# z and u of an input projection by one level of Strassen products, v computed next and kept in DRAM

## The chip, the core and the metric

The kernel runs on one core of a Trainium2 chip. Its five instruction queues work at the same time and wait for each other through semaphores: TensorE (PE: matmuls, with PEld for its weight loads), VectorE (DVE), ScalarE (ACT), GpSimd (POOL) and SyncE (SP, which here only starts DMAs). Every queue runs its instructions in the order in which the program holds them. The metric is the device time of one execution in microseconds (us), lower is better.

## The reference, cut to what matters

One decoder layer on x of 1024 tokens by 1024 columns, in f32. The change touches the first product and what uses its parts:

```python
h = x @ w_in                     # (1024, 1024) @ (1024, 2560)
q, k, v = h[:, 0:512], h[:, 512:1024], h[:, 1024:1536]
u = gelu(h[:, 1536:2048]);  z = gelu(h[:, 2048:2560])
A = dilated_attention(rope(q), rope(k), v)
B = u * (tril(w_s) @ layernorm(z) + b_s)        # 8 chunks of 128 tokens, 8 groups of 64 columns
x = LN1(alpha * x + concat(A, B) @ w_o)
# then a gated feed-forward, LN2, a gated per-layer input, LN3
```

## The kernel before, in words

Every f32 product is made of three matmuls (`mm3`, lines 131 to 134): each operand is split into a high part, which ACT copies in a matmul type (`copy`, line 111), and a low part, the rest, which DVE or POOL subtracts (`split`, line 117); the matmuls are high by high, high by low and low by high. Such a triple on 128 by 128 by 512 is called a group below.

Tokens come in eight tiles of 128. The transposed x is loaded in two halves of the 1024 contracted columns (kh 0 and 1) and four pairs of token tiles (tp 0 to 3), 512 KB each (`load_x`, line 193). The weight w_in comes in five blocks of 512 columns (4 is z, 3 is u, 2 is v, 1 is k, 0 is q) and four slices of 256 contracted rows, 512 KB each (`load_w`, line 125). All split parts of x stay in SBUF until q is done.

The order of the dense work on PE is: z (64 groups, into all eight PSUM banks), u (64 groups, pair by pair through `dense_pair`; the spatial gating `gmlp(0)` and two transposes `gm_T` are woven into its last quarter), the half of the output projection that needs only B (`wo_low`), v (64 groups), k, q, and then attention. While u is computed, DVE and ACT normalise z (`z_norm`: statistics, a power on POOL, two DVE operations, a split), eight times. v is split from PSUM straight into the tiles VL and VP. The work is laid out by hand: the program's text sets the order in each queue (`manual_schedule`), and buffers of a pool are taken in turn, so that a taker waits for the last reader of the buffer before. Pools that matter here: `raw` (2 buffers of 4 KB per partition, for loads), `w` (12, for split weights), `pg` (24 pages), `L` (3 large ones); in PSUM `A` (2 buffers of two banks: zA, ups, vps, kps), `B` (2 banks), `D0` and `D1`.

Of the kernel before, what the change touches and what calls it, by code (L numbers as in the profile page):

```python
# [30 lines left out]
DM = 1024  # L31
# [20 lines left out]
def hybrid_layer(ctx, tc, x, xT, pT, pos, w_in, ln_z_g, ln_z_b, w_sT, b_sT, w_o,  # L52
# [14 lines left out]
    def page(shape, dt, name):  # L67
        return pool.tile(shape, dt, name=name, tag="pg", bufs=24)

    def wpage(shape, dt, name):  # L70
        return pool.tile(shape, dt, name=name, tag="w", bufs=12)

    def rawpage(shape):
        return pool.tile(shape, F32, name="raw", tag="raw", bufs=2)
# [40 lines left out]
    def split(hi, lo, src, hi_eng=ACT, lo_eng=DVE):  # L115
        copy(hi_eng, hi, src)
        lo_eng.tensor_tensor(lo, src, hi.bitcast(F32), OP.subtract)  # L117

    def load_w(src, shape, name, hi_eng=ACT, lo_eng=POOL, parts=1, alloc=wpage):
        raw = rawpage(shape)  # L120
        hi = alloc(shape, F32R, name + "h")
        lo = alloc(shape, F32R, name + "l")
        n = shape[1] // parts
        for q in range(parts):
            SP.dma_start(raw[:, q * n:(q + 1) * n], src[:, q * n:(q + 1) * n])
        for q in range(parts):
            sl = slice(q * n, (q + 1) * n)
            split(hi[:, sl], lo[:, sl], raw[:, sl], hi_eng, lo_eng)
        return hi, lo
# [6 lines left out]
    def bcast(dst, vec, n, eng=SP):  # L136
        eng.dma_start(dst, bass.AP(tensor=vec.tensor, offset=vec.offset, ap=[[0, 128], [1, n]]))
        return dst
# [40 lines left out]

    x1acc_d = dram.tile([NT, 128, DM], F32, name="x1acc_d")  # L180
    x1_d = dram.tile([NT, 128, DM], F32, name="x1_d")
    hid_d = dram.tile([NG, 128, 7, 512], F32, name="hid_d")

    xh = [[None] * 4 for _ in range(2)]
    xl = [[None] * 4 for _ in range(2)]

    def load_x(kh, tp, parts=1):
        raw = page([128, 4, 256], F32, "xraw")
        xh[kh][tp] = page([128, 4, 256], F32R, "xh")
        xl[kh][tp] = page([128, 4, 256], F32R, "xl")  # L190
        st = 4 // parts
        for k in range(0, 4, st):
            SP.dma_start(raw[:, k:k + st, :], xT[kh, tp, :, k:k + st, :])
        for k in range(0, 4, st):
            split(xh[kh][tp][:, k:k + st, :], xl[kh][tp][:, k:k + st, :], raw[:, k:k + st, :])

    def xs(a, k, i):
        return a[k // 4][i // 2][:, k % 4, (i % 2) * 128:(i % 2 + 1) * 128]

    class Loader:  # L200
        def __init__(self, srcs, shape, name, lo_eng=POOL):
# [10 lines left out]
    def group(g, lo_eng=DVE):  # L212
        return Loader([w_in[g, s] for s in range(4)], [128, 2, 512], "wi", lo_eng)

    W = []
    raw0, raw1 = rawpage([128, 2, 512]), page([128, 4, 256], F32, "xraw")
    W.append((wpage([128, 2, 512], F32R, "wih"), wpage([128, 2, 512], F32R, "wil")))
    xh[0][0], xl[0][0] = page([128, 4, 256], F32R, "xh"), page([128, 4, 256], F32R, "xl")
    SP.dma_start(raw0[:, 0:1], w_in[4, 0][:, 0:1])
    SP.dma_start(raw1[:, 0:1], xT[0, 0, :, 0:1, :])  # L220
    SP.dma_start(raw0[:, 1:2], w_in[4, 0][:, 1:2])
    for k in range(1, 4):
        SP.dma_start(raw1[:, k:k + 1], xT[0, 0, :, k:k + 1, :])
    split(W[0][0][:, 0:1], W[0][1][:, 0:1], raw0[:, 0:1])
    split(xh[0][0][:, 0:1], xl[0][0][:, 0:1], raw1[:, 0:1])
    split(W[0][0][:, 1:2], W[0][1][:, 1:2], raw0[:, 1:2])
    for k in range(1, 4):
        split(xh[0][0][:, k:k + 1], xl[0][0][:, k:k + 1], raw1[:, k:k + 1])
    W.append(load_w(w_in[4, 1], [128, 2, 512], "wi", lo_eng=DVE, parts=2))
    load_x(0, 1)  # L230
    load_x(0, 2)
    load_x(0, 3)
    W.append(load_w(w_in[4, 2], [128, 2, 512], "wi"))
    load_x(1, 0)
    load_x(1, 1)
    W.append(load_w(w_in[4, 3], [128, 2, 512], "wi"))
    load_x(1, 2)
    load_x(1, 3)

    gbz = page([128, 2, 512], F32, "gbz")  # L240
    bcast(gbz[:, 0, :], ln_z_g, 512)
    bcast(gbz[:, 1, :], ln_z_b, 512)
    SP.dma_start(ident, c_id)
    SP.dma_start(bs, b_sT)
    SP.dma_start(mask, c_mask)

    Wu = group(3, POOL)
    Wu.load(4)

    zt = [psA("zA"), psA("zA")]  # L250
    for _ in range(10):
        PE.matmul(zt[0][:, 0:512], warm[:, 0:128], warm, start=True, stop=True)
    zbanks = [zt[0][:, 0:512], zt[0][:, 512:1024], zt[1][:, 0:512], zt[1][:, 512:1024],
              psB("zB"), psB("zB2"), psD("zD"), psD("zD2")]
    for kh in range(2):
        for tp in range(4):
            for k in range(4 * kh, 4 * kh + 4):
                mh = W[k // 2][0][:, k % 2, :]
                ml = W[k // 2][1][:, k % 2, :]
                for i in (2 * tp, 2 * tp + 1):  # L260
                    mm3(zbanks[i], xs(xh, k, i), xs(xl, k, i), mh, ml, k == 0, k == KB - 1)

    W = Wu
    znh = big([128, NT, 512], F32R, "znh")
    znl = big([128, NT, 512], F32R, "znl")
    z_prev = []

    def z_norm(i, zz, stats):
        ln_dve(zz, zz, *stats, gbz[:, 0, :], gbz[:, 1, :])
        split(znh[:, i, :], znl[:, i, :], zz)  # L270

    for tp in range(4):
        z = page([128, 2, 512], F32, "z")
        if tp < 2:
            ACT.activation(z.rearrange("p a b -> p (a b)"), zt[tp], AF.Gelu)
        else:
            for t in range(2):
                ACT.activation(z[:, t, :], zbanks[2 * tp + t], AF.Gelu)
        for t in range(2):
            stats = ln_stats(z[:, t, :], 512)  # L280
            if z_prev:
                z_norm(*z_prev.pop())
            z_prev.append((2 * tp + t, z[:, t, :], stats))
    z_norm(*z_prev.pop())

    def dense_pair(j, W, pa):
        for k in range(KB):
# [8 lines left out]
        for _ in gen:  # L296
            pass

    u = big([128, NT, 512], F32, "u")
    def gmlp(ch):  # L300
        for g in range(H):
            ps = (psB if g % 2 else psD)("gps")[:, 0:256]
# [21 lines left out]

    WOL = Loader([w_o[4 + k] for k in range(4)], [128, 1024], "wol", DVE)
    for j in range(4):
        pa = psA("ups")
        g = dense_pair(j, W, pa)
        if j == 3:
            gg = gmlp(0)  # L330
            for n in range(4):
                next(g)
                next(gg)
                next(gg)
                if n % 2:
                    WOL.load(1)
            run(gg)
            next(g)
            next(g)
            WOL.load(1)  # L340
            gm_T(0)
            next(g)
            gm_T(1)
        run(g)
        if j == 0:
            wsr = rawpage([128, H, 128])
            SP.dma_start(wsr, w_sT)
            POOL.affine_select(wsr, wsr, pattern=[[0, H], [1, 128]], compare_op=OP.is_ge, fill=0.0,
                               base=0, channel_multiplier=-1)
            wsh = wpage([128, H, 128], F32R, "wsh")  # L350
            wsl = wpage([128, H, 128], F32R, "wsl")
            split(wsh, wsl, wsr)
        if j == 1:
            WOL.load(1)
        ACT.activation(u[:, 2 * j:2 * j + 2, :].rearrange("p a b -> p (a b)"), pa, AF.Gelu)

    Wv = group(2)
    Wv.load(1)
    xrs = {}

    def load_xr(i):
# [18 lines left out]
    for i in range(NT):  # L380
        if i == 1:
            run(gmlp(1))
        if i == 2:
            Wv.load(1)
        if i == 6:
            rp = page([128, 5, NT, 8], F32, "rp")
            posi, inv = rp[:, 3, 0, :].bitcast(I32), rp[:, 4, 0, :]
            SP.dma_start(posi, pos)
            bcast(inv, c_inv, 8)
        wo_low(i)  # L390
        if i + 2 < NT:
            gm_T(i + 2)
    Wv.load(2)
    ACT.dma_start(x1acc_d[NT - 1], xrs.pop(NT - 1))

    posf, ang, nn = rp[:, 0, 0, :], rp[:, 1], rp[:, 2]
# [24 lines left out]
            VP[kb] = page([128, H, 128], F32R, "VP")  # L421
        return VP[kb]

    W = Wv
    Wk = group(1)
    for j in range(4):
        pa = psA("vps")
        run(dense_pair(j, W, pa))
        if j == 1:
            Wk.load(2)  # L430
        if j == 3:
            Wk.load(2)
        for t in range(2):
            v = vs(2 * j + t)
            split(v[:, :, 0:64], v[:, :, 64:128], pa[:, t * 512:(t + 1) * 512].rearrange("p (h d) -> p h d", h=H))

    def rope(tok, j):
        tv = tok.rearrange("p a (h d) -> p a h d", h=H)
# [58 lines left out]
    post = None  # L497
    for j in range(4):
        pa = psA("kps")
        g = dense_pair(j, W, pa)  # L500
        if post is not None:
            for t in range(2):
                for _ in range(5 - 3 * t):
                    next(g)
                k_post(*post, t)
        run(g)
        if j == 1:
            Wq.load(2)
        if j == 3:
            Wq.load(2)  # L510
        tok = page([128, 2, 512], F32, "tok")
        ACT.activation(tok.rearrange("p a b -> p (a b)"), pa, AF.Copy)  # L512
        rope(tok, j)
        post = (j, tok)
# [958 lines left out]
```

## Time and profile before

| | us |
|---|---|
| median of 3 runs | 1237.49 (1237.36 to 1238.53) |
| the profiled execution, whole | 1238.62 |
| its span, first to last instruction | 1236.9 |
| PE busy | 1206.2 (98% of the span) |
| DVE busy | 836.9 (68%) |
| ACT busy | 535.1 (43%) |
| POOL busy | 480.9 (39%) |

The span is what the trace covers; the profiled execution is 1.7 us longer, outside it. Positions are microseconds from the start of the span. Matmuls are pipelined: one that is listed with 0.39 us lets the next start 0.23 us after it, so distances between starts are used below and not durations. The granted clock is a share of TensorE's full 2.4 GHz, 0.50 being 1.2 GHz.

### The profile page before, as it was taken

The page shows a single profiled execution, that of the slowest core. Times are in us where ns is not written, and L with a number is a line of the kernel's source. Part 1 is how long each engine was busy: PE and PEld are TensorE (multiplying, and loading weights), DVE is VectorE, ACT ScalarE, POOL GpSimd, SP SyncE. Part 2 cuts the span into 40 slices and gives each one's busy share as a digit, 9 for nine tenths or more (in the row PEclk, how much of TensorE's full clock was granted, in tenths as well). Part 3 has the DMA queues.
Part 4 walks back from the last instruction along what each step waited for, and adds up shares of the span by engine and source line. Part 5 has one row for each costly group of instructions (what it writes and reads, how often), then busy time and mean ns, then how long its engine had stood idle before and what let it go on. Part 6 is the DMA issues. An engine that isn't in the chain of part 4 may idle for free. (4 is left out here: it accounts for less than half of the span.)

```text
span 1236.9 us, 15751 instructions
## 1 busy us (share of the span) xinstructions
PE 1206.2 (98%) x5836; PEld 1005.6 (81%) x5836; DVE 836.9 (68%) x1248; ACT 535.1 (43%) x921; POOL 480.9 (39%) x377
## 2 busy tenths in 40 slices
PE   9999999989999988999999999999999999999997
PEld 6888888878888877888888888888878888888886
DVE  5645422347888897577866677766767985798866
ACT  5322122356866653644434444444443454641221
POOL 3300000333415375576666777667510000022443
PEclk9999999999999998999999999999999999999999
DMA  7114511200201231133123331133578534740001
GB/s 281 61 51 187 182 40 35 69 18 1 86 35 55 83 104 55 48 128 105 45 107 128 128 128 52 77 128 128 190 246 314 194 112 128 247 145 18 35 34 51
DMA packets 61004, 131.69 MB, mean 106 GB/s; under 512 B 5376, under 2 KB 23168, under 8 KB 60928
## 3 DMA queue, kind: packets, MB, share of 16 engines
q1 hardware_dynamic: 59632, 126.36, 29.8%
q10 hardware_dynamic: 1296, 4.33, 0.9%
q8 instruction: 46, 0.75, 0.2%
q14 instruction: 30, 0.25, 0.1%
HBM read 97.90 MB, written 32.77 MB: 106 GB/s over the span
## 5 line engine op out<-in xcount | busy, mean ns | idle before, releaser
L132 PE MATMUL P<-xop,wop 128*128 128x512 f32 (+1 forms) x376 | 146.5, 390 | 0.0
L134 PE MATMUL P<-xop,wop 128*128 128x512 f32 (+1 forms) x376 | 145.4, 387 | 0.0
L133 PE MATMUL P<-xop,wop 128*128 128x512 f32 (+1 forms) x376 | 145.3, 386 | 0.0
L166 POOL TENSOR_TENSOR rs<-rs,neg 128x1 f32<-128x1 f32 x24 | 20.7, 862 | 276.9 <-DVE rs L165 276.9
L117 POOL TENSOR_TENSOR wop<-s,wop 128x512 fp32r<-128x512 f32 x62 | 94.2, 1525 | 86.1 <-ACT wop L111 86.1
L117 POOL TENSOR_TENSOR wop<-raw,wop 128x512 fp32r<-128x512 f32 x64 | 101.1, 1594 | 36.1 <-ACT wop L111 36.0
L111 ACT ACTIVATE aop<-raw 128x512 fp32r<-128x512 f32 x77 | 48.2, 626 | 91.8 <-DMA raw<-hid_d 58.0
L111 ACT ACTIVATE wop<-s 128x512 fp32r<-128x512 f32 x66 | 41.3, 626 | 99.2 <-DVE s L1000 53.4
L134 PEld LDWEIGHTS P<-xop,wop 128*128 128x128 f32 x376 | 71.3, 190 | 14.2
L132 PEld LDWEIGHTS P<-xop,wop 128*128 128x128 f32 x376 | 71.5, 190 | 13.8
L133 PEld LDWEIGHTS P<-xop,wop 128*128 128x128 f32 x376 | 71.5, 190 | 13.8
L444 POOL TENSOR_TENSOR rt<-tok,cos_t 128x128 f32<-128x128 f32 x8 | 4.7, 588 | 172.7 <-ACT tok L512 166.2
L117 DVE TENSOR_TENSOR aop<-raw,aop 128x512 fp32r<-128x512 f32 x77 | 54.7, 710 | 23.8 <-ACT aop L111 23.6
L133 PE MATMUL P<-bop,aop 128*128 128x512 f32 x176 | 68.8, 391 | 0.6 <-DVE bop L117 0.6
L1075 DVE SCALAR_TENSOR_TENSOR ht<-ct,mask,ht 128x1023 f32<-128x1023 f32 x22 | 47.8, 2174 | 31.3 <-ACT ht L1074 31.3
L132 PE MATMUL P<-bop,aop 128*128 128x512 f32 x176 | 68.6, 390 | 0.0
L134 PE MATMUL P<-bop,aop 128*128 128x512 f32 x176 | 68.5, 389 | 0.0
L132 PE MATMUL D<-xop,wop 128*128 128x512 f32 (+1 forms) x176 | 66.9, 380 | 0.0
L133 PE MATMUL D<-xop,wop 128*128 128x512 f32 (+1 forms) x176 | 66.8, 379 | 0.0
L134 PE MATMUL D<-xop,wop 128*128 128x512 f32 (+1 forms) x176 | 66.8, 379 | 0.0
L111 ACT ACTIVATE wop<-raw 128x512 fp32r<-128x512 f32 x66 | 39.3, 625 | 62.1 <-DMA raw<-in_w_b_dram 41.1
L1082 POOL TENSOR_TENSOR ht<-ht,ct 128x1024 f32<-128x1024 f32 x22 | 57.2, 2601 | 14.5 <-ACT ht L1079 14.5
(322 smaller groups left out, 3479.0 us busy)
## 6 DMA issues: line engine op xcount, KB each, us to landing
raw<-hid_d SPq DMA_DIRECT2D x35, 512.0 KB, 3.8
hid_d<-ct SPq DMA_DIRECT2D x22, 512.0 KB, 5.7
wd<-in_w_down_dram SPq DMA_DIRECT2D x44, 256.0 KB, 5.7
raw<-in_w_in_dram SPq DMA_DIRECT2D x18, 512.0 KB, 4.5
hid_d<-ht SPq DMA_DIRECT2D x33, 256.0 KB, 4.7
raw<-in_w_a_dram SPq DMA_DIRECT2D x11, 512.0 KB, 4.1
raw<-in_w_b_dram SPq DMA_DIRECT2D x11, 512.0 KB, 6.6
wraw<-in_w_a_dram SPq DMA_DIRECT2D x11, 512.0 KB, 5.7
```

Of the source, the lines that this page charges most:

```text
L111: ACT.activation(dst, src, AF.Copy)
L117: lo_eng.tensor_tensor(lo, src, hi.bitcast(F32), OP.subtract)
L132: PE.matmul(ps, sh, mh, start=first, stop=False, skip_group_check=chain)
L133: PE.matmul(ps, sh, ml, start=False, stop=False, skip_group_check=chain)
L134: PE.matmul(ps, sl, mh, start=False, stop=last, skip_group_check=chain)
L166: POOL.tensor_tensor(rs, rs, neghalf, OP.pow)
L444: POOL.tensor_tensor(r[:, 0], x1, cb, OP.mult)
L1075: DVE.scalar_tensor_tensor(t[:, 1:S], c[:, 0:S - 1], cw[:, f, 1:2], t[:, 1:S], op0=OP.mult, op1=OP.add)
L1082: POOL.tensor_tensor(tt[g, e], tt[g, e], ctile[g, 1, e], OP.mult)
```

## The change

z and u together are a product of x (1024 by 1024) with the 1024 columns of blocks 4 and 3. The change computes it by one level of Strassen products (the form with seven products and shared sums). The rows of the 2 by 2 split are even and odd token tiles, its inner halves are kh 0 and 1, its columns are z ("11" and "21") and u ("12" and "22"). Each of the seven products is 16 groups; `ZCHAIN` gives the PSUM chain into which it adds and `ZOUT` the output that is taken from that chain after it.

- In order, the x operands are: x(kh 0, even), x(kh 1, even), S1 = odd kh 0 + odd kh 1, S2 = S1 - even kh 0, S3 = odd kh 1 - S2 (as the text computes it, from a22 and the tile that holds S2), S4 = even kh 1 - S2, and x(kh 1, odd); the weight operands are W11, W21, T1 = W12 - W11, T2 = W22 - T1, T3 = W22 - W12, W22 and W21 - T2. The sums are made by DVE from the raw tiles, in place, four of 128x512 for each S and two of 128x1024 for each T, and every sum is then split by ACT and DVE.
- The raw x of kh 0 is loaded into the tile u, raw weights into the pool `w`. POOL makes no low parts of weights there any more.
- Products are added up in SBUF: PSUM chains are copied out by ACT or added by DVE (`zu_evac`).
- v follows at once, by `dense_pair` in the pool `A`, with `gmlp(0)` woven into its last quarter; z is normalised before and during v. v leaves PSUM by an ACT copy and a DMA into `v_d`, and is read back and split while k is computed (`v_split`).
- The odd token tiles of kh 0, whose raw data the sums have overwritten, are read a second time from xT (256 KB for each tp) after the last product's text.

The core of the diff (a line of dots stands for what is left out):

```diff
+    v_d = dram.tile([4, 128, DM], F32, name="v_d")
...
+    def s_split(n, tp):
+        if n > 2:
+            d = sop[n + 1, tp] = page([128, 2, 4, 128], F32R, "zs")
+            split(d[:, 0], d[:, 1], s3raw(tp) if n == 3 else raw_x(1, tp, 0))
+            return
...
+        d = sop[n + 1][:, tp]
+        split(d[:, 0], d[:, 1], raw_x(0, tp, 2 - n))
...
+    zu_product(1)
...
+    for j in range(4):
+        zu_evac(0, j)
+    for tp in range(4):
+        s_sum(1, tp)
+        s_split(1, tp)
+    for s_ in range(2):
+        DVE.tensor_tensor(wraw["11", s_], wraw["12", s_], wraw["11", s_], OP.subtract)
+        split_wraw(2, "11", s_)
+        if s_ == 0:
+            for j in range(4):
+                zu_evac(1, j)
+    zu_product(2)
+    for tp in range(4):
+        s_sum(2, tp)
+        s_split(2, tp)
...
+    t_sum("11", "22", "11", 0)
+    split_wraw(3, "11", 0)
+    t_sum("11", "22", "11", 1)
+    split_wraw(3, "11", 1)
+    zu_product(3)
...
+    zu_product(6)
     for tp in range(4):
+        r = rawpage([128, 4, 128])
+        SP.dma_start(r, xT[0, tp, :, :, 128:256])
+        put_x(0, 2 * tp + 1, r)
+    Wv = group(2)
+    for j in range(4):
+        ACT.activation(u[:, 2 * j, :], u[:, 2 * j, :], AF.Gelu)
+    Wv.load(3)
+    z_norm(0)
+    z_norm(2)
+    for j in range(4):
+        zu_evac(6, j)
+    Wv.load(1)
...
-        pa = psA("ups")
+        pa = psA("vps")
         g = dense_pair(j, W, pa)
...
-        ACT.activation(u[:, 2 * j:2 * j + 2, :].rearrange("p a b -> p (a b)"), pa, AF.Gelu)
+        vt = page([128, 1024], F32, "vt")
+        copy(ACT, vt, pa)
+        ACT.dma_start(v_d[j], vt)
```

The DVE queue behind the last split of x and weights that come straight from a load, before (xl and wil are low parts, z the activated z, st and mv its statistics):

```order
L117 TENSOR_TENSOR xl_152<-xraw_150,xh_151 128x1024
L117 TENSOR_TENSOR xl_164<-xraw_162,xh_163 128x1024
L117 TENSOR_TENSOR xl_170<-xraw_168,xh_169 128x1024
L158 BN_STATS st_416<-z_414 128x6
L163 BN_AGGR mv_418<-st_416 128x2
L165 TENSOR_SCALAR rs_420<-mv_418 128x1
L158 BN_STATS st_423<-z_414 128x6
L163 BN_AGGR mv_425<-st_423 128x2
L165 TENSOR_SCALAR rs_427<-mv_425 128x1
L170 SCALAR_TENSOR_TENSOR z_414<-z_414,mv_418,gbz_174 128x512
L171 SCALAR_TENSOR_TENSOR z_414<-z_414,rs_420,gbz_174 128x512
L117 TENSOR_TENSOR znl_413<-z_414,znh_412 128x512
```

The same place in the changed program (u_88 holds raw x and the sums, zs_293 is S1 split, wraw the raw weights and T1, z_284 to z_290 the partial z; the last row reads the bank of the second product):

```order
L117 TENSOR_TENSOR wil_221<-wraw_107,wih_220 128x1024
L325 TENSOR_TENSOR u_88<-u_88,raw_103 128x4x128
L117 TENSOR_TENSOR zs_293<-u_88,zs_293 128x512
L325 TENSOR_TENSOR u_88<-u_88,xraw_105 128x4x128
L117 TENSOR_TENSOR zs_293<-u_88,zs_293 128x512
L325 TENSOR_TENSOR u_88<-u_88,xraw_109 128x4x128
L117 TENSOR_TENSOR zs_293<-u_88,zs_293 128x512
L325 TENSOR_TENSOR u_88<-u_88,xraw_111 128x4x128
L117 TENSOR_TENSOR zs_293<-u_88,zs_293 128x512
L362 TENSOR_TENSOR wraw_89<-wraw_276,wraw_89 128x1024
L117 TENSOR_TENSOR wil_307<-wraw_89,wih_306 128x1024
L308 TENSOR_TENSOR z_284<-z_284,B_224 128x512
```

Where the statistics of z stood now stand, in turn, a sum and the low part of that sum, and behind all of them the weight sum and the first addition from PSUM.

The ACT queue before, where z leaves PSUM (wih are high parts of u's weights, zA_204 and zA_205 the banks of z, znh the high part of the normalised z):

```order
L111 ACTIVATE wih_193<-raw_192 128x1024
L111 ACTIVATE wih_199<-raw_198 128x1024
L275 ACT_TABLE_LOAD
L275 ACTIVATE z_414<-zA_204 128x1024
L111 ACTIVATE znh_412<-z_414 128x512
L275 ACTIVATE z_434<-zA_205 128x1024
L111 ACTIVATE znh_412<-z_414 128x512
L111 ACTIVATE znh_412<-z_434 128x512
L278 ACTIVATE z_458<-B_216 128x512
L278 ACTIVATE z_458<-B_217 128x512
```

The ACT queue of the changed program, behind the last product (wih_712, wih_718, wih_724 and wih_756 are the four slices of v's weight, zA_144 and zA_145 the banks in which the last product ends, vps_761 the first banks of v):

```order
L111 ACTIVATE wih_712<-raw_711 128x1024
L111 ACTIVATE wih_718<-raw_717 128x1024
L111 ACTIVATE wih_724<-raw_723 128x1024
L111 ACTIVATE znh_633<-z_284 128x512
L111 ACTIVATE znh_633<-z_286 128x512
L304 ACTIVATE z_284<-zA_144 128x512
L304 ACTIVATE z_286<-zA_144 128x512
L304 ACTIVATE z_288<-zA_145 128x512
L304 ACTIVATE z_290<-zA_145 128x512
L111 ACTIVATE wih_756<-raw_755 128x1024
L111 ACTIVATE znh_633<-z_284 128x512
L111 ACTIVATE znh_633<-z_286 128x512
```

The copies that empty zA_144 and zA_145 stand behind two high parts of normalised z, and these behind three slices of v's weight. vps_761 takes the buffer of zA_144.

## Rows read from the trace of the kernel before

**Rows 1.** Windows: length, PE, PEld, DVE, ACT, POOL busy (count), clock, DMA, GB/s.
```profile
0.00:40.00 40.00, 37.90 (x155) 28.03 (x155) 17.08 (x20) 21.25 (x24) 15.71 (x13) 1.00 0.72 252
40.00:80.00 40.00, 40.00 (x178) 33.14 (x177) 25.49 (x47) 11.76 (x17) 8.14 (x9) 1.00 0.12 39
```

**Rows 2.** Timeline of PE: start, duration, engine, line, operation, tiles.
```profile
4.57 0.58 PE L132 MATMUL zA<-wih,xh 128*128 128x512 f32 x1
...
18.24 0.39 PE L132 MATMUL B<-wih,xh 128*128 128x512 f32 x1
...
98.30 0.40 PE L132 MATMUL D<-wolh,gm 128*128 128x512 f32 x1
...
148.47 0.39 PE L132 MATMUL vps<-wih,xh 128*128 128x512 f32 x1
...
191.99 0.39 PE L132 MATMUL kps<-wih,xh 128*128 128x512 f32 x1
```

**Rows 3.** Timeline of ACT; in brackets idle time before and what ended it.
```profile
8.59 0.63 ACT L111 ACTIVATE wih<-raw 128x512 fp32r<-128x512 f32 x1 [0.29 <-DMA raw<-in_w_in_dram]
...
20.94 1.06 ACT L111 ACTIVATE xh<-xraw 128x1024 fp32r<-128x1024 f32 x1 [0.21 <-DMA xraw<-in_xT_dram]
...
35.99 1.28 ACT L275 ACT_TABLE_LOAD   x1
...
58.61 1.07 ACT L278 ACTIVATE z<-D 128x512 f32<-128x512 f32 x2
```

**Rows 4.** Timeline of DVE while z is normalised.
```profile
43.62 0.69 DVE L158 BATCH_NORM_STATS2 st<-z 128x6 f32<-128x512 f32 x1 [0.22 <-ACT z L275]
...
44.57 0.15 DVE L165 TENSOR_SCALAR rs<-mv 128x1 f32<-128x1 f32 x1
...
45.49 0.75 DVE L171 SCALAR_TENSOR_TENSOR z<-z,rs,gbz 128x512 f32<-128x512 f32 x1
46.94 0.69 DVE L117 TENSOR_TENSOR znl<-z,znh 128x512 fp32r<-128x512 f32 x1 [0.70 <-ACT znh L111]
47.55 0.69 DVE L158 BATCH_NORM_STATS2 st<-z 128x6 f32<-128x512 f32 x1
```

**Rows 5.** Timeline of ACT and then DVE: splits of 512 KB slices of weights.
```profile
99.42 1.05 ACT L111 ACTIVATE wih<-raw 128x1024 fp32r<-128x1024 f32 x1
...
100.51 1.22 DVE L117 TENSOR_TENSOR wil<-raw,wih 128x1024 fp32r<-128x1024 f32 x1 [2.07 <-ACT wih L111]
...
149.28 2.35 DVE L117 TENSOR_TENSOR wil<-raw,wih 128x1024 fp32r<-128x1024 f32 x2
```

**Rows 6.** Groups of DVE instructions by line: busy us, mean ns, idle before.
```profile
L995 DVE TENSOR_TENSOR s<-wraw,raw 128x512 f32<-128x512 f32 x20 | 34.6, 1731 | 0.7
...
L1000 DVE TENSOR_TENSOR s<-wraw 128x512 f32<-128x512 f32 x22 | 14.9, 681 | 0.0
```

**Rows 7.** DMA issues: queue, count, size, median us from issue to landing.
```profile
raw<-in_w_in_dram SPq DMA_DIRECT2D x18, 512.0 KB, 4.5
...
raw<-in_w_o_dram SPq DMA_DIRECT2D x8, 512.0 KB, 3.6
...
raw<-hid_d SPq DMA_DIRECT2D x7, 256.0 KB, 2.8
```

**Rows 8.** Timeline of POOL: the power in a normalisation of z.
```profile
44.80 0.99 POOL L166 TENSOR_TENSOR rs<-rs,neg 128x1 f32<-128x1 f32 x1 [3.28 <-DVE rs L165]
```

**Rows 9.** Timeline of PE behind its longest gap.
```profile
476.63 1.08 PE L898 MATMUL B<-ident,tc 128*128 128x128 f32 x4 [3.80 <-DVE tc L870]
```

**Rows 10.** Windows behind that gap.
```profile
476.00:478.00 2.00, 1.37 (x7) 1.40 (x8) 1.18 (x2) 0.25 (x1) 0.00 (x0) 0.50 0.46 186
...
480.00:482.00 2.00, 2.00 (x12) 2.00 (x11) 1.66 (x4) 1.71 (x5) 0.80 (x1) 0.54 0.00 0
482.00:484.00 2.00, 2.00 (x19) 2.00 (x19) 0.67 (x2) 0.97 (x4) 2.00 (x2) 1.00 0.04 8
```

**Rows 11.** Timeline of ACT: the second table of the rotary embedding.
```profile
155.43 0.26 ACT L410 ACTIVATE cos_t<-rp 128x64 f32<-128x64 f32 x1 [0.46 <-DVE rp L409]
```

## Prediction before the run

> **What bounds the kernel now.** I read the windows of the first 80 us first, then the timeline of PE, then those of ACT and DVE beside it. In the windows the reader sees PE busy for 37.90 of the first 40 us and for all of the next 40, at full clock [rows 1]: this stretch is bound by PE, and what the other engines do lies behind it. The timeline of PE gives the price of a matmul as a distance of starts: v runs from 148.47 to 191.99, 43.52 us for 192 matmuls, 0.2267 us each, so a group of three costs 0.68 and sixteen groups 10.88 [rows 2]. The start loses a little: between 4.57 and 18.24 stand 48 matmuls, 13.67 us instead of 10.88, 2.8 lost while the first loads arrive [rows 2]. z, u, `gmlp(0)` and two transposes end at 98.30, where `wo_low` begins; 98.30 - 4.57 - 2.8 - 384 x 0.2267 leaves 3.9 for the gating and the transposes [rows 2].
>
> **What is removed on PE.** Seven products of 16 groups are 112 groups instead of 128: 48 matmuls fewer, 10.9 us. That is the whole gain, and it holds only if each product's operands are ready when the one before it ends, once in 10.9 us.
>
> **What is added beside PE, and when it is ready.** The queues run in order, so each operand's time is a sum along the DVE queue, with ACT between a sum and its low part. Prices: a sum of 128x512 on DVE 0.68 [rows 6]; a low part 0.69, the next DVE instruction starting 0.61 after it [rows 4]; between the end of what makes a value and the start of its low part 0.70, in which ACT makes the high part (45.49 + 0.75 to 46.94 [rows 4]). One S tile is thus 0.68 + 0.70 + 0.61 = 2.0, and since sum and low part alternate in the DVE queue, four do not overlap: 8.0. A slice of a T is 1.22 (two of 1024 take 2.35, so the next starts 1.13 later) + 1.17 (ACT 1.05 from 99.42, DVE from 100.51, and 0.08 to start) + 1.13 = 3.5 [rows 5].
>
> The nearest row by form, a difference of two 128x512 tiles in the feed-forward, has 1.73 where the other has 0.68 [rows 6]; these two are the bounds. I take 0.68, because the order leaves POOL nothing but a few one-column powers here. The Trainium skill says (SBUF — State Buffer, "Who interferes with whom") that a VectorE instruction with two SBUF inputs contends with a GpSimd instruction that reads SBUF, and that the later one waits. By that page the dear row is one beside GpSimd work, and the cheap price stands; were it to hold here nonetheless, the sum would be that of the last rival.
>
> Now the times, from the profile's zero:
> - The loads are the same bytes in the same order, so the last x arrives as before and ACT splits it from 20.94 [rows 3]; 0.54 later (half of the 1.07 that two activations of 512 take) ACT takes W21's second slice, 1.05, and DVE 1.22: DVE is free at 23.8 [rows 3, 5].
> - Product 0: its first two steps go as before; its third needs the whole second slice of W11, split in halves before until 9.2 [rows 3] and now as one, low part by 10.9. So its last 41 matmuls run from about 10.9 to 20.2 (later x tiles arrive in time). Product 1: 20.2 to 31.1.
> - S1: 23.8 to 31.8. T1 slice 0: 35.3. Product 2 also needs product 1's bank, which DVE empties next (an addition from PSUM, taken as a low part, 0.69): it starts at 36.0. PE waits 4.9. It ends at 46.9.
> - DVE: the other three additions to 37.7, T1 slice 1 to 41.2 (in time), S2 to 49.2, T2 slice 0 to 52.7. Product 3 in effect starts then: PE waits 5.8. It ends at 63.4.
> - T2 slice 1 to 56.2, S3 to 64.2, T3 slice 0 to 67.7. Product 4 adds to the banks that hold product 3's result, and ACT may copy them out only after the S4 sums (two of them and two copies, 2.0): start 69.7, PE waits 6.3, end 80.6.
> - Product 5 needs S4 and W22: ACT makes the high part of T3 slice 1 by 72.5, then eight activations of 0.54 and a table load of 1.28 [rows 3], 5.6, four high parts and W22's, 3.2; DVE's low part is there at 82.7. PE waits 2.1; product 5 ends at about 93.6. For product 6 everything is ready (DVE at 93.2): it ends at 104.5.
> - v. After product 5 DVE makes its last additions (+0.9 from its end) and the low parts of two reloaded x tiles (+1.5, +2.1). There are two `raw` buffers, so the third reload starts at +1.5, lands 3.0 later and is split by +6.0; only then is v's first slice loaded: 3.6, split by +12.0; the third slice takes that buffer: 3.6 and 2.4 more, +18.0. Landing is bounded by 2.8 for 256 KB and by 3.6 and 4.5 for 512 KB [rows 7]; I take 3.0 and, for a lone load, 3.6. Behind it stand the normalisations of z tiles 0 and 2. One is 1.1 to the end of its statistics (43.62 to 44.72), 1.1 for the power, 0.75 + 0.70 + 0.69, less 0.1: 4.3 [rows 4, 8]. v's first matmul needs the banks of product 6, and the two gelu copies that free them stand in ACT's queue behind the high parts of both tiles: +18.0 + 4.3 + 4.8 (to the second high part, 3.1, and three activations) = +27.1, or 120.7. PE waits 16.2 us.
>
> From there v, `gmlp(0)` and the transposes are fed: the fourth slice is split some 3 us later and needed 8 us later, and six normalisations (26 us) fit in the first three quarters of v (32.7).
>
> **The clock.** Behind a gap of 3.80 us [rows 9] PE worked at half clock from 476.63 until about 481.1 (0.50 in the first of these windows, 0.54 in that to 482, then 1.00) [rows 10]: 4.5 us of work at half rate, 2.2 lost. After the waits before products 2, 3 and 4 such a restart shortens the next wait, as DVE sets the next start; before v it does not: + 2.2. The bounds are 0 and, twice that, 4.4.
>
> **What is moved.** v's splits and its way through DRAM (2 MB out, 2 MB back) lie beside v and k on engines that idle there. The rotary tables were ready 7.2 us after v's first matmul (155.43 + 0.26 less 148.47) [rows 2, 11]; now k stands in v's place, and they are needed only after its first 10.9. I cost this at nothing; without that cover it would be at most 2 us.
>
> **The sum.** `wo_low` starts at 120.7 + 2.2 + 43.5 + 3.9 = 170.3. Before, it starts at 98.3 and v's 43.5 come later: 141.8. The difference is +28.5. The same by terms: -10.9, waits of 4.9 + 5.8 + 6.3 + 2.1 + 16.2 = 35.3, a start that loses 4.7 instead of 2.8, and the clock 2.2. The profiled execution was 1238.62 and would become 1267.1; it lies 1.1 above the median of 1237.49, and on that the forecast is **1266 us**.
>
> **Rivals.**
> - *The sums hide.* If every product's operands are ready in time and v's banks are free, only the matmuls and the start change: -10.9 + 1.9, 1228.5. It decides at 10.9 us of DVE time for each product. For it speaks that DVE was busy only 17.08 of the first 40 us [rows 1]; against it that S2 and two slices of T2 alone are 8.0 + 7.0 in a queue that cannot overtake. 4%.
> - *v is not held.* If the banks for v come free with product 6, v is bound by its weights: the first at product 5's end + 12.0 = 105.6, and 0.6 for the third. That saves 14.5 of the 16.2 and the 2.2: about 1249. For it: before, nothing waited for normalised z until the gating. Against it: the copies' place in the ACT queue. 9%.
> - *The sums are dear.* If a difference costs 1.73 [rows 6] and one of 1024 twice that, twelve S sums (12.6) and five T slices (11) on the path add 24: about 1290. It decides if DVE shares its time with POOL, which has nearly nothing here. 3%.
> - The forecast has 84%; its own range is 1255 (loads land in 2.8, no slow restart, waits between ACT and DVE a quarter shorter) to 1277 (landings of 4.5, slow restarts counted twice, some dear sums).
>
> **How the numbers follow.** The range 1248 to 1277 takes in the second rival; it leaves out the first, the last and the ends of the forecast's own range. A change of under 0.2% (2.5 us) can't be told from none. Faster is the first rival, 4%; the same needs it with some 10 us lost, 1%; slower is all else, 95%.
>
> **What would show it.** In the timeline of PE: gaps of about 5, 6 and 6 us before the third, fourth and fifth product, each ended by DVE or, for the fifth, by ACT; a gap of about 16 us before v's first matmul, ended by ACT's gelu copy. In the windows, DVE without long idle between 24 and 83 us but broken by waits of 0.7 for ACT, and the clock at 0.50 behind the gaps. In the S sums about 0.68 each. `wo_low` should start near 170, and from k on all should run as before, 28.5 later. The forecast is wrong if products 2 to 4 follow each other without a gap, or if v starts within 3 us of the last product.

## The result and the profile after

The changed kernel takes 1267.13 us (median of 4 runs, 1266.50 to 1267.88); the kernel before, run beside it, 1238.01 us (1237.36 to 1238.95). The ratio is 1.0238, with a 95% interval of 1.0225 to 1.0251: 2.4% slower, 29.1 us. The forecast was 1266 us, with waits for operands as the reason. The profiled execution took 1266.69 us with a span of 1265.0, against 1236.9 before.

The waits of PE (who waited, for whom: us in total, times, longest) up to 330 us name the places:

```profile
PE vps L132 <- ACT z L304: 16.4, 1, 16.4
PE zA L132 <- ACT wih L111: 7.5, 2, 4.4
PE zA L132 <- ACT u L111: 3.8, 1, 3.8
PE B L132 <- DVE z L308: 1.8, 1, 1.8
...
PE zA L133 <- DVE wil L117: 0.9, 2, 0.5
```

The timeline of PE, which answers to [rows 2], has them in order of time; the first row is the first matmul of product 0, the two after it stand in product 0, and then come the first matmuls of products 2, 3 (with its second) and 4, of v, of `wo_low` and of k:

```profile
5.14 0.99 PE L132 MATMUL zA<-wih,xhl 128*128 128x512 f32 x1
...
11.11 0.80 PE L132 MATMUL zA<-wih,xhl 128*128 128x512 f32 x1 [3.10 <-ACT wih L111]
12.38 0.80 PE L133 MATMUL zA<-wil,xhl 128*128 128x512 f32 x1 [0.47 <-DVE wil L117]
...
36.99 0.47 PE L132 MATMUL B<-wih,zs 128*128 128x512 f32 x1 [1.76 <-DVE z L308]
...
52.51 0.79 PE L132 MATMUL zA<-wih,zs 128*128 128x512 f32 x1 [4.36 <-ACT wih L111]
53.77 0.79 PE L133 MATMUL zA<-wil,zs 128*128 128x512 f32 x1 [0.47 <-DVE wil L117]
...
70.75 0.50 PE L132 MATMUL zA<-wih,zs 128*128 128x512 f32 x1 [3.85 <-ACT u L111]
...
121.75 0.79 PE L132 MATMUL vps<-wih,xhl 128*128 128x512 f32 x1 [16.44 <-ACT z L304]
...
171.63 0.40 PE L132 MATMUL D<-wolh,gm 128*128 128x512 f32 x1
...
221.74 0.39 PE L132 MATMUL kps<-wih,xhl 128*128 128x512 f32 x1
```

`wo_low` begins at 171.63; 141.8 would be level with before, so 29.8 us are lost by then. DVE's timeline shows how an operand is made. Sum and low part take 0.68 each as forecast, and before the low part of a tile stands an idle 0.70 for ACT (1.06 before the first one, 1.19 before that of a T slice); a tile takes 1.99 (26.63 to 28.62):

```profile
24.27 0.68 DVE L325 TENSOR_TENSOR u<-u,raw 128x512 f32<-128x512 f32 x1
...
26.63 0.69 DVE L325 TENSOR_TENSOR u<-u,xraw 128x512 f32<-128x512 f32 x1
28.01 0.69 DVE L117 TENSOR_TENSOR zs<-u,zs 128x512 fp32r<-128x512 f32 x1 [0.70 <-ACT zs L111]
28.62 0.68 DVE L325 TENSOR_TENSOR u<-u,xraw 128x512 f32<-128x512 f32 x1
...
32.61 1.22 DVE L362 TENSOR_TENSOR wraw<-wraw 128x1024 f32<-128x1024 f32 x1
35.02 1.22 DVE L117 TENSOR_TENSOR wil<-wraw,wih 128x1024 fp32r<-128x1024 f32 x1 [1.19 <-ACT wih L111]
```

And ACT's timeline shows why v starts late. The splits of v's first three weight slices are followed by the high parts of two normalised z tiles, each with some 4 us of waiting for DVE in front of it (4.16 and 3.62), and only then by the four gelu copies (L304) that empty product 6's banks:

```profile
110.63 1.06 ACT L111 ACTIVATE wih<-raw 128x1024 fp32r<-128x1024 f32 x1 [2.64 <-DMA raw<-in_w_in_dram]
115.85 0.63 ACT L111 ACTIVATE znh<-z 128x512 fp32r<-128x512 f32 x1 [4.16 <-DVE z L171]
120.10 0.63 ACT L111 ACTIVATE znh<-z 128x512 fp32r<-128x512 f32 x1 [3.62 <-DVE z L171]
120.64 2.04 ACT L304 ACTIVATE z<-zA 128x512 f32<-128x512 f32 x4
```

The windows behind the waits answer to [rows 10]. The granted clock is 0.50 in product 3 behind its wait, and at v's start until about 126:

```profile
53.00:56.00 3.00, 2.53 (x6) 1.82 (x6) 1.84 (x2) 1.04 (x1) 0.00 (x0) 0.50 0.00 0
...
121.00:126.00 5.00, 4.25 (x10) 3.38 (x11) 2.73 (x6) 2.62 (x5) 0.03 (x1) 0.50 0.03 8
126.00:128.00 2.00, 2.00 (x8) 1.60 (x8) 1.30 (x2) 0.23 (x1) 0.95 (x1) 0.81 0.87 242
```

### The profile page after: what moved, and what is told of

Same layout as the page of the kernel before. It is cut to its first block, busy times and chain, and to the rows that moved or that the text cites. A ratio compares the mean times of both kernels' runs of the same rounds, so it can differ in the third digit from the quotient of the medians.

```text
span 1265.0 us, 15813 instructions
## 1 busy us (share of the span) xinstructions
PE 1205.4 (95%) x5788; PEld 1003.3 (79%) x5788; DVE 888.1 (70%) x1319; ACT 562.8 (44%) x972; POOL 467.9 (37%) x371
## 5 line engine op out<-in xcount | busy, mean ns | idle before, releaser
L117 POOL TENSOR_TENSOR wop<-raw,wop 128x512 fp32r<-128x512 f32 x64 | 101.3, 1597 | 35.3 <-ACT wop L111 35.1
L111 ACT ACTIVATE ct<-P 128x512 f32<-128x512 f32 x68 | 40.3, 593 | 45.4 <-PE P L134 42.8
```

The lines of the kernel that those rows point to most:

```text
L111: ACT.activation(dst, src, AF.Copy)
```

## Experiments

All times are medians; "changed" is the changed kernel with 1267.13 us, "before" the kernel before with 1238 to 1239 in every comparison.

**The place of the gelu copies (e1).**

```diff
-    z_norm(0)
-    z_norm(2)
     for j in range(4):
         zu_evac(6, j)
+    z_norm(0)
+    z_norm(2)
```

> The gelu copies of z that empty product 6's banks are put ahead of the normalisations of z tiles 0 and 2 in every queue; nothing else is changed. Theory: the wait of 16.4 us before v is the place of these copies behind two normalisations. They then stand behind the high part of v's third slice alone, which ends at 111.7 in the profile of the changed kernel; two copies take 1.1, so v starts at about 112.8 instead of 121.75 and everything behind it comes 8.9 earlier: about 1258 us. Rival one, v is held by its weights or by its x tiles: v's start stays within 1 us of 121.75 and the time at 1267. Rival two, the copies themselves are late because ACT has other work in front: v's start moves by less than 4 us, 1263 or more.

Measured: 1256.05 us (1255.69 to 1256.81). v starts at 112.12, `wo_low` at 161.6.

```profile
112.12 0.80 PE L132 MATMUL vps<-wih,xhl 128*128 128x512 f32 x1 [7.48 <-ACT z L304]
```

The forecast of 112.8 holds, and both rivals fall: normalisations that v does not need held it, through the order of one queue. The wait that is left, 7.48, is v's third slice, behind whose high part the copies still stand in ACT's queue (at 110.04, the copies at 111.00). The gain is 11.1 us where 8.9 were expected; 0.7 of the difference is that this execution was ahead by as much already at product 4 (70.08 against 70.75), the rest was not followed up.

**Sums ahead of splits (e2).**

```diff
     for tp in range(4):
         s_sum(1, tp)
+    for tp in range(4):
         s_split(1, tp)
```

(the same for S2 and S3, and for the two slices of T1 and T2. T3, which the expectation names too, stayed as it was: its low part at 55.14 still has 1.21 idle before it.)

> For S1, S2 and S3 all four sums are issued ahead of the four splits, and the two slices' sums of T1, T2 and T3 ahead of their splits; the same instructions, in another order on DVE (ACT's order is unchanged). Theory: the waits before products 2 to 4 come from DVE standing idle for ACT's high part between every sum and its low part (0.70 us, twenty times). With the sums first, the high parts run beside the next sum, an S costs 4 x 0.68 + 4 x 0.69 = 5.5 instead of 8.0 and a T slice 2.4 instead of 3.5: product 2 starts near 35.5 (product 1's end and the emptying of its bank), product 3 near 46.5 with no wait, product 4 waits about 1, product 5 about 1.7; v starts at about 109 instead of 121.75: about 1254.6 us. Rival, the waits come from the amount of DVE's or ACT's work or from the wih pages and raw buffers that the sums need: waits before product 3 and 4 shrink by less than half, 1263 or more.

Measured: 1254.75 us (1254.11 to 1255.45), as the theory has it. DVE's timeline of the first S and T now has four sums, four low parts, two sums and a low part with no idle time between:

```profile
24.25 0.68 DVE L325 TENSOR_TENSOR u<-u,raw 128x512 f32<-128x512 f32 x1
24.85 1.89 DVE L325 TENSOR_TENSOR u<-u,xraw 128x512 f32<-128x512 f32 x3
26.65 2.49 DVE L117 TENSOR_TENSOR zs<-u,zs 128x512 fp32r<-128x512 f32 x4
29.06 2.35 DVE L363 TENSOR_TENSOR wraw<-wraw 128x1024 f32<-128x1024 f32 x2
31.47 1.22 DVE L117 TENSOR_TENSOR wil<-wraw,wih 128x1024 fp32r<-128x1024 f32 x1
```

Products 2 and 3 now start without a wait, at 34.76 and 45.64; product 4 waits 1.63, and inside product 5 one of 0.76 has appeared (70.84). The instructions are the same; the order alone was worth 12.4 us. So it was not the amount of work that held PE before products 2 and 3, and most of what held it before product 4, but that every low part stood right behind the sum it belongs to.

**Both edits (e6).**

> Both single edits at once: the sums ahead of the splits, and the gelu copies of z ahead of the normalisations; nothing else. Theory: the two waits are separate mechanisms that follow each other on the path, so the gains add: 11.0 us (the first edit, 1267.1 to 1256.1) and 12.4 (the second, to 1254.8) give about 1243.7, with v's start at about 100.2 (109.6 less the 9.3 to 9.7 of the first edit), still behind a wait of some 7 us that is v's third weight slice. Rival: the sums' gain was hidden in part by the later wait or the reverse, so that together they give under 18 us: 1249 or more.

Measured: 1246.38 us, 2.7 above the theory. v starts at 100.0, as expected, behind a wait of 7.7; the gains add up to 20.8 of 23.5, and the rival (under 18) falls. At `wo_low` this version is 8.8 ahead of e2 (149.7 against 158.5), where e1 was 10.0 ahead of the changed kernel (161.6 against 171.63). These 1.2 us lie in v: the low clock behind its wait lasted longer in some of the executions than in others. v's first twelve matmuls took 4.4 us in e1 and 4.2 in e2, but 5.2 in the changed kernel and 5.0 here, where 2.7 is their time at full clock. What stands behind the remaining 1.5 was not settled.

**The start (e3).**

```diff
-    load_wraw("11", 1)
+    load_wraw("11", 1, 2)      # two DMAs, and a split for each half
```

> The second slice of W11 is loaded and split in two halves again, as in the kernel before; nothing else is changed. Theory: the start lost 3.10 and 0.47 us to that slice and then ran at half clock, so that product 0 ended at about 24 instead of 20; with halves it ends near 20 again, but product 2 waits for DVE's chain of S1 and T1, which does not depend on PE, so the wait before product 2 grows from 1.8 to about 5 and the time falls by 0 to 1: 1266 to 1267 us. Rival, the loss at the start counts in full: the time falls by 3.9, to about 1263.

Measured: 1267.85 us (1266.45 to 1268.88), no gain. Product 0 ended near 22.3 instead of 24.2, and the wait before product 2 rose from 1.76 to 4.17:

```profile
37.45 0.77 PE L132 MATMUL B<-wih,zs 128*128 128x512 f32 x1 [4.17 <-DVE z L313]
```

So what PE loses at the start is paid back, all but 0.4, as a shorter wait: product 2 waits for a chain on DVE that begins with the last x tile. From the moment at which DVE is free for S1 it starts 12.34 us later here (25.11 to 37.45) and 12.72 in the changed kernel (24.27 to 36.99), where the first high part of S1 stands on ACT behind the copies of product 0's banks. The last x tile was 0.84 later in this execution, which hides the 0.4; it is not the edit, since e8 to e11, which load W11 in the same way, have DVE free at 23.8 to 23.9.

**The clock before v (e4).**

```diff
     zu_product(6)
+    dummy = ps1("B")
+    for _ in range(66):
+        PE.matmul(dummy, X[0][0][:, 0, 0, :], ..., start=True, stop=True)
```

> 66 matmuls of 128x512 without use, into a spare bank, fill 15.0 of the 16.4 us in which PE waits before v. They leave v's operands and the instructions of the other engines as they are. Theory: the 2.2 us that I charged for the clock behind the wait are real: v's first 4.6 us run at a granted clock of 0.50; with PE kept busy the clock stays at 1.00 there, v's first matmul starts at the same 121.75 and wo_low 2.3 us earlier: about 1264.8 us. Rival, the clock falls all the same or v's start is bound by what comes later (its slices): no change within 0.5, 1267.

Measured: 1265.0 us, from runs of 1261.79, 1262.66, 1267.34 and 1268.04: the spread is wider than the effect, and the median does not show a gain. The profile, which is of the execution with 1262.66, shows one: v's first matmul starts at 121.69 (121.75 in the changed kernel), the clock is 1.00 from there on, and `wo_low` starts at 169.3 instead of 171.63:

```profile
120.00:124.00 4.00, 2.44 (x11) 1.91 (x11) 1.10 (x3) 3.52 (x6) 0.00 (x0) 1.00 0.00 0
124.00:128.00 4.00, 4.00 (x20) 3.29 (x19) 3.18 (x6) 0.28 (x1) 0.99 (x1) 1.00 0.47 131
```

In this execution 2.3 us are thus what the slow clock at v's start cost; the prediction charged 2.2. The other 1.7 us by which it is shorter than the profiled changed kernel came behind `wo_low`, and whether v started at full clock in the two executions with 1267 and 1268 too is not known.

**Low parts on POOL (e7).**

```diff
-        split(d[:, 0], d[:, 1], raw_x(0, tp, 2 - n))
+        split(d[:, 0], d[:, 1], raw_x(0, tp, 2 - n), lo_eng=POOL)
```

(the same for S3 and S4.)

> The low parts of the S tiles (16 of 128x512) are made by POOL instead of DVE; the order is that of the changed kernel, and nothing else is changed. POOL takes 1.28 to 1.6 us for such a low part elsewhere in this kernel. Theory: DVE no longer alternates with ACT, so the four sums of an S run through in 2.4 us and the waits before products 2 to 4 fall much as with the sums put first: about 1255 to 1258 us. Rival (the dear sums of the prediction): a sum of two SBUF tiles on DVE beside POOL's low part of two SBUF tiles is stretched from 0.68 to 1.3 us or more, as one of the two forms in the feed-forward was, with a mean of 1.73; an S then takes 6 to 7 us or more of the 8.0 it takes now and the time stays at 1262 to 1267.

Measured: 1262.26 us (1262.20 to 1262.66), on the rival's side. DVE's sums ran through at first, but beside POOL's low parts they stretched: a T sum took 2.19, 2.31 and 2.31 instead of 1.22, and its low part up to 2.27. DVE's timeline has the last three sums of the first S, nearly all before POOL starts (26.61), then the first T sum and its low part beside POOL, and the second T sum, when POOL has nothing to do:

```profile
25.13 1.89 DVE L325 TENSOR_TENSOR u<-u,xraw 128x512 f32<-128x512 f32 x3
27.07 2.19 DVE L362 TENSOR_TENSOR wraw<-wraw 128x1024 f32<-128x1024 f32 x1
31.23 1.51 DVE L117 TENSOR_TENSOR wil<-wraw,wih 128x1024 fp32r<-128x1024 f32 x1 [1.97 <-ACT wih L111]
...
36.41 1.22 DVE L362 TENSOR_TENSOR wraw<-wraw 128x1024 f32<-128x1024 f32 x1
```

And POOL's timeline at the same time, four low parts in 7.28, 1.82 each:

```profile
26.61 7.28 POOL L117 TENSOR_TENSOR zs<-u,zs 128x512 fp32r<-128x512 f32 x4 [25.68 <-DMA wraw<-in_w_in_dram]
```

This is the mechanism of the third rival, "the sums are dear". It exists; the changed kernel escapes it because POOL has nothing to do there. On the way to product 3 it cost 3.2 us: four sums, a T sum and a low part took 3.58, 2.31 and 2.25, where e2 has 2.49, 1.22 and 1.22. What POOL's own longer low parts cost beside that was not measured apart.

**A version without the waits (e8 to e11).** Four steps, each made from what the trace of the one before still showed.

e8 takes e2 and e3, puts a T3 sum ahead of S3's splits and S4's sums ahead of T3's split (not, as the expectation has it, ahead of S3's), moves the gelu of z behind the splits for product 5, and loads three of the x tiles and v's first slice earlier; the copies of product 6 stand ahead of the normalisations.

> A version of the changed kernel without the waits that were found: sums ahead of the splits; W11's second slice in halves; S4's sums and a sum of T3 ahead of S3's splits; gelu of z behind the splits of S4 and W22; three of the four reloaded x tiles and v's first weight slice ahead of the last additions from product 5, the second slice behind product 6; gelu copies of product 6 ahead of the normalisations. Theory: if the waits were all that the change lost, products 1 to 6 follow each other with under 3 us lost, product 6 ends at about 92 and v starts at 93, 28.7 earlier than in the changed kernel, without a slow restart (2.2 more): about 1267.1 - 31 = 1236 us, 1 to 3 below the kernel before; with all waits gone it would be 1228. Rival: the engines beside PE have no room left (DVE and ACT both work nearly without a break from 24 to 80) and the waits come back elsewhere: 1243 or more, no better than the two edits together.

Measured: 1241.00 us, between theory and rival: the ratio to before is 1.0024 (1.0013 to 1.0035). v starts at 92.6, as expected, but waits again inside itself, now for its third slice, whose split stood behind the high part of a normalised tile, and the clock falls behind that:

```profile
92.62 0.50 PE L132 MATMUL vps<-wih,xhl 128*128 128x512 f32 x1 [2.44 <-ACT z L309]
...
101.64 0.79 PE L132 MATMUL vps<-wih,xhl 128*128 128x512 f32 x1 [3.29 <-ACT wih L111]
```

e9 puts all of v's slices ahead of the normalisations, and product 6's copies ahead of the slices left by then; a T1 sum and T3's split change places as the expectation says:

```diff
+    for j in range(4):
+        zu_evac(6, j)
+    Wv.load(3)
     for j in range(4):
         ACT.activation(u[:, 2 * j, :], u[:, 2 * j, :], AF.Gelu)
-    Wv.load(1)
-    for j in range(4):
-        zu_evac(6, j)
     z_norm(0)
     z_norm(2)
-    Wv.load(2)
```

> The version before this one, with the waits that its trace still shows taken away: the gelu copies of product 6 directly behind product 6 and ahead of the gelu of u and of all of v's remaining slices; v's second to fourth slice ahead of the normalisations; one sum of T1 ahead of S1's splits and the other behind the additions from product 1; T3's low part ahead of S4's sums. Theory: the waits of 2.4 and 3.3 (with 0.5) us before and in v, the 2.2 us of a slow restart behind the second of them, and 1 to 1.5 us at products 2 and 4 go: 9 to 10 us, 1241.0 to about 1231.5, 0.5 per cent below the kernel before. Rival: DVE and ACT, which are busy for 16 to 19 of every 20 us there, only move the wait to the next product or to the gating behind v: 1236 or more, no difference from the kernel before.

Measured: 1241.34 us, no gain; the theory failed and the rival held. v now starts at 89.1 without a wait, and its third pair waits 5.30 for ACT's copy of the first pair's bank:

```profile
117.40 0.80 PE L132 MATMUL vps<-wih,xhl 128*128 128x512 f32 x1 [5.30 <-ACT vt L111]
```

ACT's timeline has this copy (`vt`) behind the high parts of four normalised tiles, the first of them at 101.28 and the fourth at 114.86:

```profile
101.28 0.63 ACT L111 ACTIVATE znh<-z 128x512 fp32r<-128x512 f32 x1 [2.08 <-DVE z L171]
...
114.86 0.63 ACT L111 ACTIVATE znh<-z 128x512 fp32r<-128x512 f32 x1 [4.44 <-DVE z L171]
...
116.34 1.00 ACT L111 ACTIVATE vt<-vps 128x1024 f32<-128x1024 f32 x1
```

e10 normalises z tiles 1, 3, 4 and 6 one pair of v later, tile 5 behind `gmlp(0)`, tile 7 behind the first transposes.

> The version before this one, with the copies of v's finished banks ahead of all but two of the normalisations: z tiles 1, 3, 4 and 6 are normalised one pair of v later than in the version before, tile 5 behind gmlp(0)'s products, tile 7 behind the first two transposes; nothing else is changed. Theory: the 5.3 us that v's third pair waits there are the copy of v's first bank, which stands in ACT's queue behind the high parts of four normalised tiles, each of which waits for DVE; with the copy ahead of them this wait and the slow restart behind it (some 2.2 us) go, v runs from 89.1 to about 133 and wo_low starts near 137 instead of 146.0: about 1232 to 1234 us, 0.3 to 0.5 per cent below the kernel before. Rival: the normalisations as a whole (eight times 4.3 us on DVE with POOL and ACT between) bind, and the wait moves to gmlp(0) or the transposes: wo_low at 143 or later, 1238 or more.

Measured: 1238.53 us, ratio to before 1.000 (0.9992 to 1.0009). v has no wait but one of 0.3, and `wo_low` starts at 138.4 where 137 was expected, but the time misses 1232 to 1234: `wo_low` now loses 0.63, 0.64 and 2.73. The last is tile 7, by way of ACT: its high part stands there ahead of a copy of v and of the high part of k's first weight slice, and DVE comes to `wo_low`'s first additions (L549, at 147.42) only behind the low part of that slice. The rows are of ACT, DVE and PE:

```profile
143.23 0.63 ACT L111 ACTIVATE znh<-z 128x512 fp32r<-128x512 f32 x1 [4.38 <-DVE z L171]
...
146.27 1.23 DVE L117 TENSOR_TENSOR wil<-raw,wih 128x1024 fp32r<-128x1024 f32 x1 [1.69 <-ACT wih L111]
...
148.24 0.36 PE L132 MATMUL D<-znh,wsh 128*128 128x256 f32 x1 [2.73 <-DVE xr L549]
```

e11 makes the normalisations in pairs, as e2 did with the sums, and has all of them ahead of `gmlp(0)` again:

```diff
-    def z_norm(i):
-        zz = zp[i // 2][:, i % 2, :]
-        ln_dve(zz, zz, *ln_stats(zz, 512), ...)
-        split(znh[:, i, :], znl[:, i, :], zz)
+    def z_norm(*tiles):        # statistics of both, both normalised, both split
```

> The version before this one with the eight normalisations made in pairs: the statistics of both tiles, then both normalisations, then both splits, so that DVE works on the second tile while POOL and ACT work on the first; all four pairs end before gmlp(0). Nothing else is changed. Theory: eight single normalisations take 4.3 us each on DVE, 1.15 of it waiting for POOL (0.45) and ACT (0.70); in pairs nearly all of that goes, about 6.4 for two, and none is left to stand between wo_low's first results and their additions. wo_low then starts near 137 and k near 187.5, where the version before has 138.4 and 193.2: 4 to 6 us, 1238.5 to about 1233 to 1234.5, 0.3 to 0.4 per cent below the kernel before. Rival: with gmlp(0)'s operations behind the last pair on DVE, or with what stands behind k, the gain is given back: k not before 191 or the time not below 1237.

Measured: 1233.84 us (1231.66 to 1236.81 over 11 runs) against 1238.68, ratio 0.9963 (0.9953 to 0.9972). This version beats both kernels, by 4.8 us and by 33.3. A pair takes 6.4 us on DVE, from the start of one pair to that of the next; two single ones took 8.5 in e10 (119.13 to 127.64):

```profile
114.88 0.69 DVE L158 BATCH_NORM_STATS2 st<-z 128x6 f32<-128x512 f32 x1
...
121.32 0.69 DVE L158 BATCH_NORM_STATS2 st<-z 128x6 f32<-128x512 f32 x1
```

`wo_low` starts at 137.66 and k at 187.76 (191.99 before, [rows 2]). How much of the 4.7 us against e10 is the pairs and how much the place of tiles 5 and 7 was not measured apart. Of PE's waits this is all that is left up to 250 us beside one of 1.3 that belongs to the warm-up:

```profile
PE zA L132 <- ACT wih L111: 2.1, 3, 1.2
...
PE zA L133 <- DVE wil L117: 1.0, 2, 0.8
PE B L132 <- DVE gm L117: 0.3, 1, 0.3
PE vps L133 <- DVE wil L117: 0.3, 1, 0.3
```

## Why the prediction came out right

- **The number.** 1266 forecast, 1267.1 measured; +28.5 at `wo_low` forecast, +29.8 measured. The single starts test more than the total, since products 2 to 4 hang on one chain along DVE and v on the loads and normalisations behind product 5: product 2 at 36.99 (forecast 36.0), 3 at 52.51 with its second matmul at 53.77 (52.7), 4 at 70.75 (69.7), v at 121.75 (120.7), `wo_low` at 171.63 (170.3). All are about one us late together, and nearly all of that is there at product 2: 0.5 when DVE becomes free (24.27 instead of 23.8), and 0.4 more in the first tile of S1, whose high part stands on ACT behind the copies of product 0's banks (idle 1.06 instead of 0.70). That link from product 0's end into DVE's chain is missing in the prediction.
- **Sums, splits and their alternation.** A sum 0.68, an S tile 1.99 (2.0 forecast), a T slice 3.55 (3.5; 1.22 + 1.19 + 1.14). e2 shows that the alternation is the cause of these waits and not the work: the order alone is worth 12.4 us.
- **The waits, one by one, were mis-sized.** 1.76, 4.36 + 0.47, 3.85, none and 16.44 stand where 4.9, 5.8, 6.3, 2.1 and 16.2 were forecast: 26.9 instead of 35.3. Two terms make up for it. The start: product 0 began at 5.14 and ended at about 24.2 instead of 20.2. The forecast had counted that the second slice of W11 comes as one, but its low part was used at 12.38 and not at 10.9, which is 1.5 us, and PE then ran at a clock of 0.50 until about 17, which is 2.5 us more for the last 41 matmuls and was charged at nothing. The start thus loses 6.0 more than before, where the forecast had 1.9. And the restarts: product 3 lasted 14.4 us and product 4 12.7, not 10.9, and v lost 2.5 (171.63 - 121.75 less 43.5 and 3.9). Together -10.9 + 6.0 + 26.9 + 7.8 = 29.8: the last term is what is left for the low clock behind the waits; products 3 and 4 and v have 7.3 of it (3.5 + 1.8 + 2.5, less the 0.47 inside product 3 that is counted as a wait). The sum was safe against both errors because DVE's chain, not PE, sets the starts of products 2 to 4, as the prediction's part on the clock says. e3 shows that for the start: product 0 ended 1.9 us earlier, and product 2 gained 0.4 of it at most. For the restarts no run shows it, only the trace: product 3 ran 3.5 longer and the wait behind it was 2.5 shorter, which leaves the one us by which all starts are late.
- **Product 5's wait of 2.1** did not appear: product 4 ran 1.8 longer at a low clock (0.69 from 71 to 74), and ended at 83.4, when the low part of W22's first slice (forecast for 82.7) was just there.
- **v.** The largest term was right in size (16.44 for 16.2) and in cause, by e1. The slow start of v was right as well (2.2 charged; 2.3 by the profiled execution of e4, and between 1.5 and 2.5 for v's first twelve matmuls in the changed kernel, e1, e2 and e6).
- **Behind v.** k starts 29.75 later than before, the first `wop` matmul 28.5 (466.8 before, 495.3 after), the span ends 28.1 later: as forecast within 1.3 us. The difference falls from 29.73 at 298 to 28.49 at 365, inside the attention; PE waits there 0.7 less for `pt` and `mixf` than before, and no run shows why. That the total comes out closer than the terms is in part luck. v's way through DRAM shows no cost; no run measured it by itself.
- **The rivals.** "The sums hide" is far off; e11 shows what it takes to come near: 1233.8 against 1228.5. "v is not held" would have been 1249; e1, which takes only the normalisations out of the way, gave 1256, since the copies then still stand behind v's third slice (7.48 us). With the copies ahead of the slices, in e9, v starts without a wait. "The sums are dear" is a real mechanism (e7) without its condition. The Trainium skill (SBUF — State Buffer, "Who interferes with whom") told the two cases apart: a VectorE instruction with two SBUF inputs contends with a GpSimd instruction that reads SBUF. The runs agree: 0.68 for each of the changed kernel's sums with POOL idle, 2.19 to 2.31 instead of 1.22 beside POOL in e7.

## What to carry to other kernels

A chain that goes from one engine to another and back costs its hand-overs once per tile if the instructions are issued tile by tile, and nearly nothing if they are issued step by step over several tiles: the same instructions in that order were worth 12.4 us for the sums and 2.1 for each pair of normalisations. What empties PSUM for the next matmuls belongs in its queue ahead of everything that waits for a third engine. And removing work from the bounding engine paid here only after its operands had been timed along the in-order queues that make them: 10.9 us of matmuls were removed, and the queues of DVE, ACT and the loads had to be put in another order before 4.8 of them showed.

## What the hardware showed that was not expected

- The clock does not follow the length of a gap alone. A gap of 1.76 at 36.99 in the changed kernel left it at 1.00 in every window up to 42; a gap of 1.86 at 32.96 in e8 brought it to 0.50; one of 2.44 before v in e8 left it at 1.00; and at the start of e3, gaps of 0.66, 1.07, 0.23 and 1.12 between few matmuls ended in 0.50 as well. The windows (us) of e8 behind the 1.86:

```profile
32.00:34.00 2.00, 1.04 (x3) 0.88 (x4) 2.00 (x5) 0.08 (x1) 0.00 (x0) 0.80 0.00 0
34.00:36.00 2.00, 2.00 (x6) 1.51 (x6) 2.00 (x4) 0.00 (x0) 0.00 (x0) 0.50 0.00 0
...
38.00:40.00 2.00, 2.00 (x11) 1.62 (x10) 2.00 (x5) 0.81 (x2) 0.00 (x0) 1.00 0.00 0
```

- Contention with POOL goes both ways: POOL's low part of 128x512, 1.30 in e7 while DVE was idle (72.75), took 1.82 on average beside DVE's T sum and its low part; DVE alone made four of them in 2.4 in e2 (26.65 to 29.06).
- In the profiled execution of e4, 66 matmuls without use in a gap cost nothing that the trace shows, since nothing else used PE there, and saved 2.3 us at the next start; the median of its four runs does not show the gain.
